# A transformer block on one core: where the last gate's row lies in the w_up stage, and how far ahead Pool makes its sums

## The chip, the cores and the metric

The kernel runs on one core of a Trainium2 chip. The core has a matrix engine (PE, with its weight loads shown apart as PEld), a vector engine (DVE), an activation engine (ACT), a general engine (POOL) and a queue engine (SP) that issues most of the DMAs. Each engine executes its own instructions strictly in the order in which the program lists them and waits on semaphores where it needs another engine's result. The metric is device microseconds of one execution; lower is better.

## The reference

One diffusion block in float32 over 1024 tokens of width 1024. What matters here is its second half, the feed-forward part, with 2816 hidden columns:

```python
def swiglu(h, w_up, w_down):
    a, b = jnp.split(h @ w_up, 2, axis=-1)
    return (jax.nn.silu(a) * b) @ w_down
...
        h2 = modulate(rmsnorm(x, g_ffn[l]), mod[:, 3, None], mod[:, 4, None])
        x = x + mod[:, 5, None] * swiglu(h2, w_up[l], w_down[l])
    return rmsnorm(x, g_final)
```

`mod[:, 5]` is the last gate, one row of 1024 numbers. The kernel multiplies it into the columns of w_down ahead of the product instead of into the result.

## The kernel before

Every float32 product is made of three fast matmuls: an operand is split into a high part (a copy on ACT, L92) and the rest (a subtraction on DVE, L93), and `mm3` (L121 to L123) adds high times high, high times low and low times high. Large products go through a Strassen scheme with seven products in place of eight. Its operands are blocks and sums of blocks, named B11, T2, T3, T1, B21, T4, B22.

The change lies in the w_up stage. It goes over 22 column blocks m of w_up, and each has seven products (five for the first four, which were begun earlier): 146 products of 12 matmuls. One written loop over products g sets the order of every engine's work, with nothing left to a scheduler. In turn g it issues:

- `up_sums`: POOL's sums of blocks of w_up for a product further ahead. T2 needs s1 and s2 (L1118, L1119), T3 needs s3 (L1123), B22 needs s4 (L1126). They lie in a ring of four buffers named st.
- `up_split` for product g + 4: the copy on ACT and the subtraction on DVE. After a block's last split the two loads of w_up for block m + 2 are issued on SP.
- the 12 matmuls of product g,
- work put off from earlier turns. The gate, one turn after a block's last product: a Silu on ACT (L1176), then a product on POOL (L1177). The stores of the result.
- `up_evac(g)`: DVE reads the product's bank (L1155 for T2, L1161 for T3, L1163 for T1, L1169 for T4, L1173 for B22). ACT reads B11 (L1153) and makes a Silu of B21 (L1166). T3 and T4 use one bank, so T4's matmuls must wait until L1161 has read T3.
- from block 3 on, a step or two of `DownOperands`. It prepares the operands of w_down for the stage after: rows are loaded (L809), multiplied by the last gate (L841, one row on DVE and one on POOL), combined, and each of seven forms is split into a tile named od (copy on ACT L813, subtraction on DVE L817), which SP stores to DRAM (L821). There are eleven pairs of rows. The forms come in the order B11, T2, B22, B21, T1, T3, T4; those of the last pair stay on chip.

The tiles od come out of a ring of 32 buffers of 4 KB per partition ("slots"). The stage holds 28 of them for the latents' operands and one for the last gate's row, m5, so that three rotate among the od tiles: a copy into od waits until the store of the tile three back has landed. Another ring, gl, has six buffers of half the size; the stage uses all six for the three tiles t per pair that carry T1, T3 and T4.

Of the kernel before, what the change touches and what calls it, by code (L numbers as in the profile page):

```python
# [12 lines left out]
ALU = mybir.AluOpType  # L13
# [22 lines left out]
HS = (H0, H1)  # L36
# [7 lines left out]
def block_kernel(ctx: ExitStack, tc: tile.TileContext,  # L44
# [4 lines left out]
    load, store = nc.sync.dma_start, nc.scalar.dma_start  # L49

    x, ctxt, out = x[0], ctxt[0], out[0]
# [13 lines left out]
    def slot(name, shape=(P, T), dtype=F32):  # L65
        return slots.tile(list(shape), dtype, name=name, tag="s", bufs=NS)
# [7 lines left out]
    def ev_(name="ev"):  # L74
        return wp.tile([P, HALF], F32, name=name, tag="ev", bufs=8)

    def gl_(name="gl"):
        return wp.tile([P, HALF], F32, name=name, tag="gl", bufs=6)
# [159 lines left out]
    def dtile(name, shape=(P, T)):  # L238
        return dram.tile(list(shape), F32, name=name)
# [6 lines left out]
    m5d = dtile("m5d")  # L246
# [469 lines left out]
    for n, (ka, fa, kb, fb) in enumerate(PAIRS):  # L716
# [23 lines left out]
        if ka[0] == "ff":  # L740
            e = ev_()
            zs = (e, c12, c21, c22)
# [44 lines left out]
    DPAIRS = [(ka, kb) for a, b in SEG for ka, kb in zip(a, b)]  # L787

    def last_gate():
        z = slot("m5")  # L790
        load(out=z, in_=m5d)
        return z

    class DownOperands:

# [37 lines left out]
        def one(self, i, j, m5):  # L833
            ra, rb = self.raw[i, 0], self.raw[i, 1]
            x11, x12, x21, x22 = ra[:, H0], ra[:, H1], rb[:, H0], rb[:, H1]
            t = self.t
            nxt = self.pairs.index(i) + 1
            nxt = self.pairs[nxt] if nxt < len(self.pairs) else None
            if j < 2:
                for eng, z in ((dve, ra), (pool, rb)):  # L840
                    eng.tensor_tensor(z[:, HS[j]], z[:, HS[j]], m5[:, HS[j]], op=ALU.mult)  # L841
            elif j == 2:
                t["T1"] = self.tile_("t")
                dve.tensor_tensor(t["T1"], x12, x11, op=ALU.subtract)
            elif j == 3:
                t["T3"] = self.tile_("t")
                dve.tensor_tensor(t["T3"], x22, x12, op=ALU.subtract)
                self.hi(i, "B11", x11)
            elif j == 4:
                dve.tensor_tensor(x12, x22, t["T1"], op=ALU.subtract)  # L850
            elif j == 5:
                self.lo(i, "B11")
                self.hi(i, "T2", x12)
            elif j == 6:
                t["T4"] = self.tile_("t")
                dve.tensor_tensor(t["T4"], x21, x12, op=ALU.subtract)
            elif j == 7:
                self.lo(i, "T2")
                if nxt is not None:
                    self.fetch(nxt, 0)  # L860
                self.hi(i, "B22", x22)
            elif j == 8:
                self.lo(i, "B22")
                self.hi(i, "B21", x21)
            elif j == 9:
                self.lo(i, "B21")
                if nxt is not None:
                    self.fetch(nxt, 1)
                self.hi(i, "T1", t["T1"])
            elif j < 12:  # L870
                nm, then = (("T1", "T3"), ("T3", "T4"))[j - 10]
                self.lo(i, nm)
                self.hi(i, then, t[then])
            else:
                self.lo(i, "T4")
# [171 lines left out]
    for h_ in range(2):  # L1047
# [16 lines left out]
        for n in range(4):  # L1064
            z = slot("xr")
# [3 lines left out]
        for k in range(4):  # L1069
            for m in (EARLY[k] if h_ else ()):  # L1070
                early.append(up_pair(m).head(True, m > 1, psum if m > 1 else None, gl_))
            if h_ == 0:
                fz = slot("F0", (P, 2, HALF))
                zs = [fz[:, 0, :], fz[:, 1, :]]
                F0.append(zs)
            else:
                zs = [ev_("z12"), ev_("z22")]
# [10 lines left out]
    LEAD = 4  # L1088
# [9 lines left out]
    def up_loads(m):  # L1098
        u = UP[m] = UpState()
        u.p = early[m] if m < len(early) else None  # L1100
        if u.p is not None and u.p.ra is not None:
            u.ra = u.p.ra
        else:
            u.ra = load_cols(w_up, m * P, KT)
        u.rb = load_cols(w_up, DFF + m * P, KT)
        u.o = {}
        u.a = dict(B11=u.ra[:, H0], B21=u.ra[:, H1], T4=u.rb[:, H1])

    def up_sums(g):
        m, nm = prods[g]  # L1110
        u = UP[m]
        a11, a12, a21, a22 = u.ra[:, H0], u.ra[:, H1], u.rb[:, H0], u.rb[:, H1]

        def st():
            return wp.tile([P, HALF], F32, name="st", tag="st", bufs=4)
        if nm == "T2":
            s1, s2 = st(), st()
            pool.tensor_tensor(s1, a21, a22, op=ALU.add)  # L1118
            pool.tensor_tensor(s2, s1, a11, op=ALU.subtract)  # L1119
            u.a["T1"], u.a["T2"] = s1, s2  # L1120
        elif nm == "T3":
            s3 = u.a["T3"] = st()
            pool.tensor_tensor(s3, a11, a21, op=ALU.subtract)  # L1123
        elif nm == "B22":
            s4 = u.a["B22"] = st()
            pool.tensor_tensor(s4, a12, u.a["T2"], op=ALU.subtract)  # L1126

    def up_split(g):
        m, nm = prods[g]
        UP[m].o[nm] = wop(UP[m].a[nm])  # L1130

    def up_product(g):
        m, nm = prods[g]
        u = UP[m]
        if nm in ("B11", "T2") and not hasattr(u, "bank"):
            p = u.p if u.p is not None else up_pair(m)
            u.bank = dict(zip("YZW", (f() for f in p.banks[1:])))
            u.bank["X"] = u.p.X if u.p is not None else p.banks[0]()
            u.m1 = u.p.m1 if u.p is not None else ev_("m1")
        ps = u.bank[dict(B11="X", T2="Y", T3="W", T1="Z", B21="X", T4="W", B22="Z")[nm]]  # L1140
        first = nm in ("B11", "T2", "T3", "T1")
        for k in range(4):
            mm3(ps, hl(u.o[nm], blk(k)), hl(G[nm][k]), first and k == 0, k == 3, not first)
# [4 lines left out]
    def up_evac(g):  # L1148
        m, nm = prods[g]
        u = UP[m]  # L1150
        b = u.bank
        if nm == "B11":
            act.copy(u.m1, b["X"])  # L1153
        elif nm == "T2":
            dve.tensor_tensor(u.m1, b["Y"], u.m1, op=ALU.add)  # L1155
            if u.p is not None:
                u.e = ev_()
                act.activation(u.e, b["X"], AF.Silu)
        elif nm == "T3":
            u.u3 = ev_("u3")  # L1160
            dve.tensor_tensor(u.u3, b["W"], u.m1, op=ALU.add)  # L1161
        elif nm == "T1":
            dve.tensor_tensor(u.u3, b["Z"], u.u3, op=ALU.add)  # L1163
        elif nm == "B21":
            u.e = ev_()
            act.activation(u.e, b["X"], AF.Silu)  # L1166
        elif nm == "T4":
            c21 = ev_("c21")
            dve.tensor_tensor(c21, b["W"], u.m1, op=ALU.add)  # L1169
            dve.tensor_tensor(u.e, u.e, c21, op=ALU.mult)  # L1170
            later(g + 1, lambda: store(out=Gd[m // 2][:, m % 2, H0], in_=u.e))
        else:
            dve.tensor_tensor(u.m1, b["Z"], u.m1, op=ALU.add)  # L1173

            def gate():
                act.activation(u.m1, u.m1, AF.Silu)  # L1176
                pool.tensor_tensor(u.m1, u.m1, u.u3, op=ALU.mult)  # L1177
            later(g + 1, gate)
            later(g + 2, lambda: store(out=Gd[m // 2][:, m % 2, H1], in_=u.m1))

    N = len(prods)
    made = DownOperands(list(range(1, len(DPAIRS))) + [0], gl_)
    first_made = prods.index((3, "T2"))
    with tc.manual_schedule():
        up_loads(0)
        up_loads(1)
        m5 = last_gate()
        for g in range(-LEAD - 1, N + 3):
            if 0 <= g + LEAD + 1 < N:
                up_sums(g + LEAD + 1)  # L1190
            if 0 <= g + LEAD < N:
                up_split(g + LEAD)
                m = prods[g + LEAD][0]
                if ends[m] == g + LEAD and m + 2 < NFF:
                    up_loads(m + 2)
            if 0 <= g < N:
                up_product(g)
            for fn in todo_at.pop(g, ()):
                fn()
            if 0 <= g < N:  # L1200
                up_evac(g)
            if g >= first_made:
                made.step((g + 1 - first_made) / (N + 2 - first_made), m5)
        made.step(1, m5)
# [154 lines left out]
    for s in range(len(SEG)):  # L1359
        segment(s, O, gs)  # L1360
        for t in RES.get(s, ()):
            for ch in range(2):
                z = gl_("xh")
# [32 lines left out]
```

## Time and profile before

| | us |
|---|---|
| median of 3 runs | 1546.57 (1545.77 to 1548.61) |
| the profiled execution | 1543.4 |
| its span, first instruction to last | 1541.7 |
| PE busy in the span | 1461.0 (95%) |
| DVE busy | 1127.9 (73%) |
| ACT busy | 715.5 (46%) |
| POOL busy | 600.9 (39%) |

A share of busy time is a mean over stages. In the rows below a stretch or an instruction is given by its start from the span's start. The bracket behind an instruction is the time for which its engine sat idle ahead of it, and what ended that.

### The profile page before, as it was taken

Reading aid. Unit: us, or ns where it says so; the run is one execution under the profiler, and the core shown is the slowest. Engines: PE = TensorE matmul, PEld = TensorE weight load, DVE = VectorE, ACT = ScalarE, POOL = GpSimd, SP = SyncE. Lnnn points to the kernel's source line nnn. Section 1 sums busy time; section 2 is a strip of 40 time slices with the busy share of each in tenths; the row PEclk is TensorE's granted clock in tenths of the full one; section 3 lists DMA queues with packets and bytes.
Section 4 is the critical chain, followed back from the end, with each engine's and each line's share of the span. In section 5 each row is a group of like instructions: output and inputs, shape, how many; then the busy total and the mean of one; then the engine's idle time right before and its main releaser. Section 6 shows DMA issues by size and latency. Waiting matters only on the chain.

```text
span 1541.7 us, 19297 instructions
## 1 busy us (share of the span) xinstructions
PE 1461.0 (95%) x6754; PEld 1196.2 (78%) x6754; DVE 1127.9 (73%) x1552; ACT 715.5 (46%) x1207; POOL 600.9 (39%) x402
## 2 busy tenths in 40 slices
PE   6998999999899999999999979999999999999997
PEld 6887788777677777888788757778778777788886
DVE  2456686888877657685736777888898889777786
ACT  4355655766433332234326543334343334767635
POOL 0033143434232224253512644445555454544456
PEclk9799999999999999999999989999999999999999
DMA  9343432334667748931645232566666656699922
GB/s 304 107 149 121 140 110 66 126 115 151 216 208 253 239 159 269 326 141 41 228 155 180 94 96 96 198 228 232 224 222 220 204 189 228 217 350 361 326 78 110
DMA packets 206931, 288.11 MB, mean 187 GB/s; under 512 B 11409, under 2 KB 131826, under 8 KB 206834
## 3 DMA queue, kind: packets, MB, share of 16 engines
q1 hardware_dynamic: 181778, 238.64, 47.5%
q10 hardware_dynamic: 25056, 48.25, 8.4%
q8 instruction: 53, 0.87, 0.2%
q14 instruction: 44, 0.36, 0.1%
HBM read 199.80 MB, written 87.03 MB: 186 GB/s over the span
## 4 chain that ended last, share of the span: by engine, by line
PE 46%; DVE 15%; issue 13%; DMA 11%; POOL 8%; ACT 6%; SPq 1%; ACTq 0%; POOLq 0%; DVEq 0%
PE acc L121 8%; PE acc L123 8%; PE acc L122 8%; DVE op L93 4%; PE aux L121 4%; PE aux L122 4%; PE aux L123 4%; DMA raw<-in_w_mod_dram 4%; PE aux L316 2%; DMA raw<-in_w_in_dram 1%; POOL rawd L841 1%; DMA OdB<-od 1%; ACT op L92 1%; DMA OdT<-od 1%; POOL st L1126 1%
## 5 line engine op out<-in xcount | busy, mean ns | idle before, releaser
L93 DVE TENSOR_TENSOR op<-raw,op 128x512 fp32r<-128x512 f32 x208 | 195.6, 945 | 100.6 <-ACT op L92 98.3
L92 ACT CAST op<-raw 128x512 fp32r<-128x512 f32 x216 | 131.7, 619 | 161.2 <-PE acc L123 99.9
L93 DVE TENSOR_TENSOR op<-st,op 128x512 fp32r<-128x512 f32 x160 | 144.4, 904 | 40.2 <-ACT op L92 39.3
L121 PE MATMUL acc<-T,op 128*128 128x512 f32 x400 | 159.9, 400 | 13.6 <-ACT T L92 6.1
L121 PE MATMUL aux<-T,op 128*128 128x512 f32 x400 | 158.5, 396 | 12.2 <-DVE u L1161 7.7
L92 ACT CAST op<-st 128x512 fp32r<-128x512 f32 x160 | 96.9, 618 | 146.3 <-POOL st L1119 27.3
L122 PE MATMUL acc<-T,op 128*128 128x512 f32 x400 | 159.2, 398 | 4.0 <-DVE T L93 4.0
L123 PE MATMUL acc<-T,op 128*128 128x512 f32 x400 | 157.9, 395 | 0.0
L122 PE MATMUL aux<-T,op 128*128 128x512 f32 x400 | 157.1, 393 | 0.0
L123 PE MATMUL aux<-T,op 128*128 128x512 f32 x400 | 156.2, 392 | 0.0
L121 PE MATMUL aux<-B,op 128*128 128x512 f32 x300 | 118.1, 394 | 5.9 <-DVE u L190 4.7
L121 PE MATMUL acc<-B,op 128*128 128x512 f32 x300 | 117.6, 393 | 3.0 <-ACT m L165 1.8
L123 PE MATMUL acc<-B,op 128*128 128x512 f32 x300 | 117.5, 392 | 1.6 <-DVE op L93 1.6
L122 PE MATMUL aux<-B,op 128*128 128x512 f32 x300 | 117.0, 390 | 0.0
L122 PE MATMUL acc<-B,op 128*128 128x512 f32 x300 | 116.9, 390 | 0.0
L123 PE MATMUL aux<-B,op 128*128 128x512 f32 x300 | 116.9, 390 | 0.0
L1177 POOL TENSOR_TENSOR m<-m,u 128x512 f32<-128x512 f32 x22 | 34.3, 1559 | 180.4 <-ACT m L1176 180.4
L121 PEld LDWEIGHTS acc<-T,op 128*128 128x128 f32 x400 | 76.5, 191 | 34.8 <-ACT T L92 8.0
L121 PEld LDWEIGHTS aux<-T,op 128*128 128x128 f32 x400 | 75.7, 189 | 33.2 <-issue 8.5
L181 POOL TENSOR_TENSOR st<-raw 128x512 f32<-128x512 f32 x18 | 32.6, 1812 | 170.3 <-DMA raw<-in_w_in_dram 127.3
L122 PEld LDWEIGHTS acc<-T,op 128*128 128x128 f32 x400 | 76.5, 191 | 21.3 <-DVE T L93 5.5
L123 PEld LDWEIGHTS acc<-T,op 128*128 128x128 f32 x400 | 76.3, 191 | 16.0 <-issue 0.2
(387 smaller groups left out, 3602.9 us busy)
## 6 DMA issues: line engine op xcount, KB each, us to landing
raw<-in_w_in_dram SPq DMA_DIRECT2D x60, 512.0 KB, 5.1
raw<-in_w_up_dram SPq DMA_DIRECT2D x46, 512.0 KB, 6.4
OdT<-od SPq DMA_DIRECT2D x40, 512.0 KB, 4.2
so<-OdT SPq DMA_DIRECT2D x40, 512.0 KB, 5.7
raw<-in_w_mod_dram SPq DMA_DIRECT2D x32, 512.0 KB, 4.9
OdB<-od SPq DMA_DIRECT2D x30, 512.0 KB, 4.9
so<-OdB SPq DMA_DIRECT2D x30, 512.0 KB, 6.5
rawd<-in_w_down_dram SPq DMA_DIRECT2D x22, 512.0 KB, 5.7
```

What stands on the lines that cost most here:

```text
L92: (act.copy if hi_eng is act else hi_eng.tensor_copy)(h, v)
L93: t_last[0] = lo_eng.tensor_tensor(l, v, h.bitcast(F32), op=ALU.subtract)
L121: pe.matmul(ps, lh, rh, start=first, stop=False, skip_group_check=cont)
L122: pe.matmul(ps, lh, rl, start=False, stop=False, skip_group_check=cont)
L123: pe.matmul(ps, ll, rh, start=False, stop=last, skip_group_check=cont)
L181: pool.tensor_tensor(s1, a21, a22, op=ALU.add)
L316: pe.matmul(ps[:, 2 * i:2 * i + 2], wm[f][i][:, blk(k)], sc[:, k, :], start=k == 0, stop=k == KT - 1)
L841: eng.tensor_tensor(z[:, HS[j]], z[:, HS[j]], m5[:, HS[j]], op=ALU.mult)
L1126: pool.tensor_tensor(s4, a12, u.a["T2"], op=ALU.subtract)
L1177: pool.tensor_tensor(u.m1, u.m1, u.u3, op=ALU.mult)
```

## The change

The last gate's row is loaded as two halves into two buffers of the ring gl, and later: two turns ahead of the first step of `DownOperands` instead of ahead of the loop. The slot that it held joins the rotation, so that the od tiles have four buffers in place of three, and the tiles t have four in place of six. POOL's sums are issued for product g + 6 in place of g + 5.

```diff
     def last_gate():
-        z = slot("m5")
-        load(out=z, in_=m5d)
-        return z
+        zs = [gl_("m5") for _ in HS]
+        for z, s in zip(zs, HS):
+            load(out=z, in_=m5d[:, s])
+        return zs
...
-                    eng.tensor_tensor(z[:, HS[j]], z[:, HS[j]], m5[:, HS[j]], op=ALU.mult)
+                    eng.tensor_tensor(z[:, HS[j]], z[:, HS[j]], m5[j], op=ALU.mult)
...
         up_loads(0)
         up_loads(1)
-        m5 = last_gate()
-        for g in range(-LEAD - 1, N + 3):
-            if 0 <= g + LEAD + 1 < N:
-                up_sums(g + LEAD + 1)
+        for g in range(-LEAD - 2, N + 3):
+            if g == first_made - 2:
+                m5 = last_gate()
+            if 0 <= g + LEAD + 2 < N:
+                up_sums(g + LEAD + 2)
```

The lists of PE, DVE and ACT stay as they were, name for name. POOL's list moves. From the gate of block 4 (L1177 on m1_7721) to the next gate it reads before as follows; st from L1126 is s4, from L1118 and L1119 s1 and s2, from L1123 s3, and L841 is the last gate's product with a half row of w_down:

```order
L1177 TENSOR_TENSOR m1_7721<-m1_7721,u3_7783 128x512
L841 TENSOR_TENSOR rawd_7811<-rawd_7811,m5_7267 128x512
L1126 TENSOR_TENSOR st_7905<-raw_7601,st_7790 128x512
L841 TENSOR_TENSOR rawd_7811<-rawd_7811,m5_7267 128x512
L1118 TENSOR_TENSOR st_7953<-raw_7769 128x512
L1119 TENSOR_TENSOR st_7954<-st_7953,raw_7767 128x512
L1123 TENSOR_TENSOR st_7974<-raw_7767,raw_7769 128x512
L1177 TENSOR_TENSOR m1_7886<-m1_7886,u3_7947 128x512
```

And after, POOL over the same stretch, with the sum s4 of the block before ahead of the gate (lines from here on stand one or two lower in the file):

```order
L1127 TENSOR_TENSOR st_7881<-raw_7607,st_7767 128x512
L1178 TENSOR_TENSOR m1_7725<-m1_7725,u3_7789 128x512
L842 TENSOR_TENSOR rawd_7815<-rawd_7815,m5_7559 128x512
L842 TENSOR_TENSOR rawd_7815<-rawd_7815,m5_7560 128x512
L1119 TENSOR_TENSOR st_7930<-raw_7775 128x512
L1120 TENSOR_TENSOR st_7931<-st_7930,raw_7773 128x512
L1124 TENSOR_TENSOR st_7959<-raw_7773,raw_7775 128x512
L1127 TENSOR_TENSOR st_8041<-raw_7773,st_7931 128x512
L1178 TENSOR_TENSOR m1_7890<-m1_7890,u3_7953 128x512
```

The sum s4 has moved from behind a gate to ahead of it, and behind the two L841 that stand there in other blocks. On SP, at the start of the stage, the gate's row stood between the second halves of the first two w_up blocks and the loads of the third:

```order
L103 DMA raw_7265<-in_w_up_dram 128x8x128
L791 DMA m5_7267<-m5d_156 128x1024
L103 DMA raw_7296<-in_w_up_dram 128x8x128
L103 DMA raw_7298<-in_w_up_dram 128x8x128
L103 DMA raw_7397<-in_w_up_dram 128x8x128
```

After, it comes in two halves behind the loads of block 4:

```order
L103 DMA raw_7265<-in_w_up_dram 128x8x128
L103 DMA raw_7296<-in_w_up_dram 128x8x128
L103 DMA raw_7298<-in_w_up_dram 128x8x128
L103 DMA raw_7397<-in_w_up_dram 128x8x128
L103 DMA raw_7399<-in_w_up_dram 128x8x128
L103 DMA raw_7501<-in_w_up_dram 128x8x128
L103 DMA raw_7503<-in_w_up_dram 128x8x128
L792 DMA m5_7559<-m5d_156 128x512
L792 DMA m5_7560<-m5d_156 128x512
L103 DMA raw_7607<-in_w_up_dram 128x8x128
```

Six loads of w_up have moved ahead of the gate's row. The only other move on SP is at the end of the stage, where the first load of a stored form (so, L1233) stands ahead of the last row of w_down and one od store instead of behind them.

## Rows read from the trace of the kernel before

**Rows 1.** Windows: busy us and (instructions) by engine, PE clock, DMA share, GB/s.

```profile
950.00:1000.00 50.00, 47.12 (x198) 38.28 (x199) 43.19 (x52) 18.81 (x34) 22.40 (x14) 0.97 0.49 172
...
1150.00:1200.00 50.00, 49.99 (x220) 40.83 (x219) 45.97 (x56) 19.63 (x35) 23.55 (x15) 1.00 0.66 220
...
1350.00:1400.00 50.00, 50.00 (x222) 41.20 (x221) 39.67 (x57) 36.17 (x46) 24.45 (x19) 1.00 0.99 351
```

**Rows 2.** The page: a matmul's group; count, busy us, mean ns, idle before.

```profile
L122 PE MATMUL aux<-B,op 128*128 128x512 f32 x300 | 117.0, 390 | 0.0
```

**Rows 3.** PE's waits from 900 to 1330: total us, times, longest.

```profile
PE aux L121 <- DVE u L1161: 7.7, 5, 2.2
...
PE acc L121 <- DVE u L1161: 2.8, 2, 2.2
PE acc L121 <- ACT op L1310: 2.3, 1, 2.3
PE acc L121 <- DVE u L1163: 1.1, 2, 0.7
```

**Rows 4.** Waits of all engines, 850 to 1320.

```profile
POOL m L1177 <- ACT m L1176: 179.7, 21, 14.8
ACT od L813 <- DMA OdT<-od: 49.5, 10, 9.9
ACT od L813 <- DMA OdB<-od: 42.2, 17, 6.2
DVE op L93 <- ACT op L92: 40.1, 19, 5.3
```

**Rows 5.** Timeline of PE, two resumptions.

```profile
950.30 0.47 PE L121 MATMUL aux<-T,op 128*128 128x512 f32 x1 [0.55 <-DVE u L1161]
...
991.49 0.47 PE L121 MATMUL aux<-T,op 128*128 128x512 f32 x1 [2.18 <-DVE u L1161]
```

**Rows 6.** Timeline of DVE ahead of the second.

```profile
967.50 0.68 DVE L93 TENSOR_TENSOR op<-raw,op 128x512 fp32r<-128x512 f32 x1
...
974.66 0.69 DVE L93 TENSOR_TENSOR op<-st,op 128x512 fp32r<-128x512 f32 x1 [5.28 <-ACT op L92]
...
976.18 0.69 DVE L93 TENSOR_TENSOR op<-st,op 128x512 fp32r<-128x512 f32 x1 [0.23 <-ACT op L92]
...
979.78 0.69 DVE L93 TENSOR_TENSOR op<-st,op 128x512 fp32r<-128x512 f32 x1 [0.98 <-ACT op L92]
980.39 0.68 DVE L1173 TENSOR_TENSOR m<-acc,m 128x512 f32<-128x512 f32 x1
...
983.90 1.77 DVE L93 TENSOR_TENSOR op<-raw,op 128x512 fp32r<-128x512 f32 x1
```

**Rows 7.** Timeline of ACT, same stretch.

```profile
973.49 0.62 ACT L813 CAST od<-t 128x512 fp32r<-128x512 f32 x1 [9.86 <-DMA OdT<-od]
```

**Rows 8.** Timeline of SP: store of the pair's first form; and of its second.

```profile
958.53 0.34 SPq L821 DMA_DIRECT2D OdB<-od  x1
...
965.81 1.96 SPq L821 DMA_DIRECT2D OdT<-od  x1
```

**Rows 9.** The tile od: its stores, from issue to landing.

```profile
DMA to landing us min/median/max: 2.6/4.5/8.7
```

**Rows 10.** Timeline of POOL: same stretch, and a late product on w_down's row.

```profile
981.82 1.61 POOL L1177 TENSOR_TENSOR m<-m,u 128x512 f32<-128x512 f32 x1 [14.79 <-ACT m L1176]
...
985.08 1.74 POOL L1126 TENSOR_TENSOR st<-raw,st 128x512 f32<-128x512 f32 x1
...
1256.92 2.55 POOL L841 TENSOR_TENSOR rawd<-rawd,m 128x512 f32<-128x512 f32 x2 [6.90 <-DMA rawd<-in_w_down_dram]
1265.09 1.61 POOL L1177 TENSOR_TENSOR m<-m,u 128x512 f32<-128x512 f32 x1 [5.63 <-ACT m L1176]
```

**Rows 11.** Windows of 10 us behind two of PE's waits.

```profile
990.00:1000.00 10.00, 8.51 (x30) 6.88 (x31) 9.92 (x14) 3.73 (x7) 3.49 (x3) 0.83 0.27 97
...
1130.00:1140.00 10.00, 7.79 (x28) 6.26 (x28) 9.94 (x13) 4.32 (x8) 4.29 (x3) 0.83 0.48 149
```

## The prediction

> **What bounds the kernel now.** Start with the table of windows. In the w_up stage PE is busy 49.99 of 50 us where nothing disturbs it, with 220 matmuls, so one starts every 0.227 us; in a disturbed window of the same length it starts 198 and its clock is 0.97 [rows 1]. PE is the bound, and only what it loses in this stage can be won. The groups of the page say that a matmul's record lasts 0.390 us [rows 2], 0.163 us longer than the distance to the next start, so each wait in the view of waits is really 0.16 us longer than shown.
>
> Then PE's waits. Two reasons make up the stage's loss: DVE's L1161, which must have read T3's bank before T4 may write it (7.7 + 2.8 us in seven waits), and L1163, the same for the other bank (1.1 us in two). Together 11.6 us in nine waits, with the correction 11.6 + 9 x 0.163 = 13.1 us [rows 3]. The next view is the clock behind the two longest of these waits: 0.83 over ten microseconds, twice [rows 11]. That is (1 - 0.83) x 10 = 1.7 us each, a short spell at 1.2 instead of 2.4 GHz after PE stood for some 2.2 us; together 3.4 us. So the stage holds 13.1 + 3.4 = 16.5 us at the most.
>
> Now why DVE reads late. DVE works for 43 to 46 of 50 us here [rows 1], so it cannot make up lost time quickly. In the timeline of DVE ahead of PE's wait of 2.18 us [rows 5] there is a hole of 5.28 us, which an ACT copy ended [rows 6]. ACT itself had stood for 9.86 us at a copy into od, until a store of an earlier od tile landed [rows 7]. Summed over the stage, ACT stands 49.5 + 42.2 = 91.7 us for od stores and DVE 40.1 us for ACT's copies [rows 4]. After the hole DVE reads block m's last bank (L1173) at 980.39; only then come the Silu and the gate on POOL, at 981.82 after 14.79 us of idling [rows 10]. Everything that POOL still owes stands behind that gate and comes in one burst. While POOL works, a DVE subtraction takes 1.77 us where it takes 0.68 us alone [rows 6]. So the lateness that ACT began is doubled by POOL's burst just ahead of L1161.
>
> **The change part by part.** *The fourth od buffer.* A copy into od now waits for the store four back. The copy at 973.49 is the pair's fifth; ACT was free for it at 973.49 - 9.86 = 963.63 [rows 7]. It waited for the second form's store, issued at 965.81; now it needs only the first's, issued at 958.53 [rows 8]. Stores land 2.6 to 8.7 us after issue [rows 9], so that one is there by 961.1 to 967.2: a wait of 0 to 3.6 us for 9.86. The sixth copy now meets the second's store, at the same 973.4, but ahead of it ACT has already made the fifth copy and the operand copy that DVE lacked. So DVE does in its hole the subtraction for the operand (0.69 us) and that for od (0.68 us by its like [rows 6]). The two later holes of 0.23 and 0.98 us came from ACT's catching up [rows 6] and go with it. L1173 comes 0.69 + 0.68 + 0.23 + 0.98 = 2.6 us sooner, and with it the gate and the burst. PE's wait there was 2.18 + 0.16 = 2.3 us: it goes, with 0.3 us to spare. The bounds for this part: none of the 16.5 us, if the wait only passes to the sixth copy, and all of it.
>
> *The sums a product earlier.* POOL's number of sums stays. But s4, 1.74 us, ran inside the burst at 985.08 [rows 10]; by the new list it stands ahead of the gate, in the 14.79 us in which POOL idled. That takes up to 1.77 - 0.68 = 1.09 us of slowed DVE work out of each burst, and s1 to s3 come a place earlier. Bounds: 0 and seven L1161 waits x 1.09 = 7.6 us; within the sum it serves the same waits as the buffer, so I add nothing for it.
>
> *What it costs.* The tiles t have four buffers for three a pair. A buffer is asked for again six steps after its last reader at the earliest (T3's at step 3 takes the buffer whose last reader was T1's step 10 of the pair before). There are 143 steps in 133 turns of 12 x 0.227 = 2.7 us, so that is 15 us, and I take nothing; without that cover DVE would stand. The gate's row is issued two turns, 5.4 us, or more ahead of its first reader, the first L841, and the median landing of a twice as large store is 4.5 us [rows 9]: nothing; at worst 8.7 - 5.4 = 3.3 us, once. On SP one more load stands ahead of the last row of w_down: its issue, and at worst its landing of up to 8.7 us by the stores, once, at the last pair, whose sums no longer stand behind that row; taken as nothing. Nothing is added to PE's, DVE's or ACT's lists.
>
> *The sum.* Not all of the 13.1 us goes. The first wait, 0.55 us at 950.30 [rows 5], has no od copy ahead of it; it is what a burst alone costs, a quarter of the 2.2 us of the large ones. I let a quarter of all stay: 13.1 x 0.75 = 9.8 us won. The clock's 3.4 us I count in full, since no wait near 2.2 us should be left. Gain 13.2 us: the profiled execution goes from 1543.4 to 1530.2 us. Before's median lies 3.17 us above that execution, so the forecast for the median is 1546.57 - 13.2 = 1533.4 us. The stage behind takes the gain over whole, since PE is busy 50.00 of 50 us there, though the DMA engines are at 0.99 [rows 1]. What is late next is DVE itself at 46 of 50 us. PE's 2.3 us at the stage's end, where the next stage's first operands are late (L1310) [rows 3], I leave as they are; they could go as well, since the loads of that stage queue on SP behind buffers that s4 frees.
>
> **The rivals.** *The burst alone decides.* POOL's work is not less, and each of its sums still makes a DVE subtraction 1.09 us longer [rows 6]. The Trainium skill ("SBUF — State Buffer", section "SBUF: two separate sides") calls the ports that the two share an exclusive lock: the later of two such instructions waits for all of the first. By that rule moving sums wins no DVE time at all, it only chooses which DVE instruction is hit. The trace's 0.68 and 1.77 us agree. As a mechanism here: the buffer brings nothing since DVE, slowed as much as before, falls behind in every burst; only s4's leaving shortens seven waits by half to all of 1.09 us, 3.8 to 7.6 us, middle 5.7, and the clock still falls: 1546.57 - 5.7 = 1540.9 us. For it speaks that a wait without any od copy exists (950.30). Against it, that the large waits follow a hole of DVE's. Chance 0.20.
>
> *The wait only moves.* The sixth copy waits for the landing at 973.4 as the fifth did, what stands behind it in ACT's list comes no sooner, and PE's waits stay within a microsecond or two: about 1545.5 us. For it: the store itself lands no earlier. Against it: five instructions are ahead of that landing now. Chance 0.12.
>
> *Slower: s4 behind late rows of w_down.* In the new list two L841 stand ahead of s4 in several blocks, and L841 waits for a row of w_down: at 1256.92 it had waited 6.90 us, and the gate came at 1265.09 [rows 10]. Between the end of that pair, 1256.92 + 2.55 = 1259.47, and the gate there are 5.6 us, of which s4 takes 1.74, so 3.9 us of slack. If a row lands over 3.9 us later, s4 and the gate behind it are late, then the split that needs s4, then DVE's reads. From the fastest to the slowest landing of an od store, as large as a row's load, there are 6.1 us [rows 9], so a late one costs 6.1 - 3.9 = 2.2 us; at four of ten pairs 8.8 us, less the 5.7 us of the burst: 1546.57 + 3.1 = 1549.7 us. Against it: for that the buffer must bring nothing, and SP is asked for nothing more. Chance 0.05.
>
> **How the numbers follow.** Most of PE's waits go: 0.63, at 1533.4 us. Its own range runs from all of it and the stage's end too, 1546.57 - 16.5 - 2.3 = 1527.8 us, to half of it, 1538. The range for 8 in 10 takes in the first rival and part of the second, 1528 to 1543.5 us. What a measurement of this kernel can tell from no change is 0.2%, 3.1 us. Faster by more: the forecast and nearly all of the first rival, 0.82; within it: the second and a rest, 0.12; slower: 0.06, the last rival and what I don't see.
>
> **What would show it.** Right: ACT's waits for od stores fall from 91.7 to below 50 us, DVE's for ACT's copies from 40.1 to below 25, PE's for L1161 from 10.5 to below 4; no window of the stage has a clock of 0.83; the sums s4 lie in POOL's idle time, and POOL's longest wait for the gate's Silu is shorter than 14.8 us. Wrong: PE's waits on L1161 of about 2 us still there behind bursts of POOL, with ACT's od waits gone (the first rival); ACT's od waits as long as before, now at the sixth copy (the second); ACT's copies waiting for s4 behind an L841 that waits for its row (the third). If PE's waits are gone and the time is not, the stage behind gave it back, and its waits would show where.

## The result, and the profile after

The changed kernel takes 1528.78 us (median of 4 runs, 1528.64 to 1530.2) against 1546.84 us for the kernel before on the same chip: a ratio of 0.9891, interval 0.9874 to 0.9907. It is 18 us faster; the forecast was 13.2. The profiled execution takes 1530.2 us with a span of 1528.5, 13.2 us less than the one of before, so that the sum, which was made against one profiled execution, came out to the tenth. That is in part luck, as the stage itself shows. Its first and last marks in PE's timeline stand below: PE's wait for T at the stage's entry and its wait for an operand of the next stage. First before (columns: start, duration, engine, line, operation, operands, and the idle time ahead with what ended it):

```profile
900.88 0.80 PE L121 MATMUL acc<-T,op 128*128 128x512 f32 x1 [3.16 <-ACT T L92]
...
1321.77 0.50 PE L121 MATMUL acc<-od,op 128*128 128x512 f32 x1 [2.31 <-ACT op L1310]
```

The same two of after, and between them the only two matmuls of PE that still wait:

```profile
902.75 0.80 PE L121 MATMUL acc<-T,op 128*128 128x512 f32 x1 [3.15 <-ACT T L92]
...
953.46 0.47 PE L121 MATMUL aux<-T,op 128*128 128x512 f32 x1 [0.55 <-ACT op L92]
...
1260.64 0.47 PE L121 MATMUL aux<-T,op 128*128 128x512 f32 x1 [1.87 <-DVE u L1162]
...
1307.86 0.60 PE L121 MATMUL acc<-od,op 128*128 128x512 f32 x1 [2.06 <-ACT op L1312]
```

From mark to mark the stage took 420.89 us and takes 405.11: 15.8 us less. The execution after entered the stage 1.9 us later than that of before and took 0.7 us more behind it, which leaves 13.2. A second profile of either kernel (below) gives 420.18 and 404.53 us, a difference of 15.7, while the entry of these four lies anywhere from 899.50 to 902.75. The stage's gain is thus firm, and the entry varies by itself.

The view of waits over the w_up stage answers to [rows 4], PE's part of it to [rows 3] (total us, times, longest):

```profile
POOL m L1178 <- ACT m L1177: 149.9, 22, 12.4
...
ACT od L814 <- DMA OdT<-od: 26.5, 8, 4.7
...
DVE op L93 <- ACT op L92: 23.9, 13, 4.0
...
ACT od L814 <- DMA OdB<-od: 9.8, 6, 4.1
...
PE aux L121 <- DVE u L1162: 1.9, 1, 1.9
```

ACT's waits for stores of od fell from 91.7 to 36.3 us, DVE's for ACT's copies from 40.1 to 23.9, PE's for the two banks from 12.0 to 1.9 (the prediction added up 11.6 and left out a line of 0.4). POOL's longest wait for the gate's Silu is 12.4 us, and the clock is 1.00 from 950 to the wait at the stage's end, so the signs that the prediction gave for being right are there. The windows answer to [rows 1]:

```profile
950.00:1000.00 50.00, 49.45 (x218) 40.62 (x217) 45.88 (x55) 18.40 (x33) 23.50 (x15) 1.00 0.50 174
...
1150.00:1200.00 50.00, 50.00 (x222) 41.39 (x221) 47.80 (x55) 20.92 (x38) 27.29 (x17) 1.00 0.61 200
```

The disturbed window holds 218 matmuls instead of 198, and its clock is 1.00 instead of 0.97. DVE works 45.88 of 50 us where it worked 43.19: it does the same work with fewer holes. How the first large wait of [rows 5] went can be followed along ACT, DVE and POOL; SP's issue of the second store of that pair is now at 967.81 where it was at 965.81 [rows 8], so some 2 us are to be taken off to compare places. ACT's timeline, the fifth and the sixth copy of the pair, answers to [rows 7]:

```profile
965.02 0.62 ACT L814 CAST od<-t 128x512 fp32r<-128x512 f32 x1
965.72 0.62 ACT L92 CAST op<-st 128x512 fp32r<-128x512 f32 x1
...
975.37 0.62 ACT L814 CAST od<-t 128x512 fp32r<-128x512 f32 x1 [1.95 <-DMA OdT<-od]
```

The fifth copy no longer waits, and the operand copy that DVE lacked follows it at once. The landing that the fifth met is now met by the sixth, after 1.95 us instead of 9.86. DVE's timeline answers to [rows 6], POOL's to [rows 10]:

```profile
976.54 0.69 DVE L93 TENSOR_TENSOR op<-st,op 128x512 fp32r<-128x512 f32 x1 [3.60 <-ACT op L92]
...
979.68 0.68 DVE L1174 TENSOR_TENSOR m<-acc,m 128x512 f32<-128x512 f32 x1
...
989.99 0.68 DVE L1162 TENSOR_TENSOR u<-aux,m 128x512 f32<-128x512 f32 x1
```

```profile
968.09 1.29 POOL L1127 TENSOR_TENSOR st<-raw,st 128x512 f32<-128x512 f32 x1 [0.69 <-DVE op L93]
...
981.11 1.60 POOL L1178 TENSOR_TENSOR m<-m,u 128x512 f32<-128x512 f32 x1 [11.73 <-ACT m L1177]
```

L1174 reads the last bank at 979.68, set back by those 2 us 977.7 where it was 980.39: 2.7 us sooner, where 2.6 were worked out. The sum s4 (L1127) has left the burst for POOL's idle time, as forecast. But from the gate to the read of T3's bank (L1162) there are 989.99 - 981.11 = 8.9 us, as before (990.67 - 981.82 = 8.9). Over the stage's blocks the median of this stretch is 7.2 us in both kernels. The wait went since all of this came sooner, not since the burst became shorter.

### The profile page after: what moved, and what is told of

Its sections match the earlier page's. It is cut to its first block, busy times and chain, and to the rows that moved or that the text cites. A ratio compares the mean times of both kernels' runs of the same rounds, so it can differ in the third digit from the quotient of the medians.

```text
span 1528.5 us, 19338 instructions
## 1 busy us (share of the span) xinstructions
PE 1459.4 (95%) x6754; PEld 1199.1 (78%) x6754; DVE 1131.6 (74%) x1552; ACT 714.4 (47%) x1207; POOL 599.4 (39%) x402
## 5 line engine op out<-in xcount | busy, mean ns | idle before, releaser
L92 ACT CAST op<-raw 128x512 fp32r<-128x512 f32 x216 | 131.9, 619 | 178.0 <-PE acc L123 105.2
L92 ACT CAST op<-st 128x512 fp32r<-128x512 f32 x160 | 96.8, 618 | 118.0 <-DVE ev L1171 20.0
```

Of the source, the lines that this page charges most:

```text
L92: (act.copy if hi_eng is act else hi_eng.tensor_copy)(h, v)
```

## The experiments

The length of the stage between the two marks serves beside the time, since it leaves out how late an execution enters it. Each time stands beside the kernel before on the same chip.

**e1_slot** and **e2_sums**: each part of the change alone. e1 takes the sums back to one product ahead; e2 is the kernel before with only the sums two ahead.

```diff
 # e1_slot, against after
-        for g in range(-LEAD - 2, N + 3):
+        for g in range(-LEAD - 1, N + 3):
-            if 0 <= g + LEAD + 2 < N:
-                up_sums(g + LEAD + 2)
+            if 0 <= g + LEAD + 1 < N:
+                up_sums(g + LEAD + 1)
 # e2_sums, against before
-            if 0 <= g + LEAD + 1 < N:
-                up_sums(g + LEAD + 1)
+            if 0 <= g + LEAD + 2 < N:
+                up_sums(g + LEAD + 2)
```

> The change without its second part: the last gate's row in two half-size buffers, four od buffers, POOL's sums one product ahead as before. Theory (ACT's waits for od stores start the chain, so the buffer carries the gain): most of it is here, 10 to 15 us of the changed kernel's 18 below before, so 1532 to 1537 us; ACT's waits for od stores fall to about 40 us as in the changed kernel, and PE's waits on DVE's L1161 fall from 10.5 to under 5 us. Rival (POOL's burst behind the gate decides, the buffer brings nothing): under 5 us below before, 1542 us or more, with PE's waits on L1161 still about 10 us although ACT's od waits are down.

> The change without its first part: POOL's sums two products ahead, the gate's row in its old slot, three od buffers. Theory: ACT's od waits stay at some 90 us and with them most of PE's waits; s4's leaving the burst wins 3 to 6 us, so 1541 to 1544 us. Rival (the burst decides): this carries the gain, 10 us or more, 1537 us or less, with ACT's od waits unchanged.

e1: 1527.61 us, 0.989 (0.9868 to 0.9911); e2: 1545.72 us, 1.0006 (0.9989 to 1.0024). The buffer alone brings the whole gain, more than the 10 to 15 us expected; the sums alone bring nothing that can be measured, where 3 to 6 us were expected. The waits of e1 are those of after, or lower:

```profile
DVE op L93 <- ACT op L92: 21.2, 15, 3.8
ACT od L814 <- DMA OdT<-od: 18.7, 9, 3.1
...
ACT od L814 <- DMA OdB<-od: 9.3, 5, 5.3
...
PE aux L121 <- DVE u L1162: 1.0, 2, 0.5
```

Why do the sums bring nothing, although s4 goes where it was sent? The timeline of DVE, POOL and PE in e2 ahead of a wait of 3.38 us:

```profile
1255.28 2.55 POOL L841 TENSOR_TENSOR rawd<-rawd,m 128x512 f32<-128x512 f32 x2 [8.70 <-DMA rawd<-in_w_down_dram]
...
1257.79 1.75 POOL L1126 TENSOR_TENSOR st<-raw,st 128x512 f32<-128x512 f32 x1
1258.31 1.79 DVE L817 TENSOR_TENSOR od<-t,od 128x512 fp32r<-128x512 f32 x1
...
1264.57 1.61 POOL L1177 TENSOR_TENSOR m<-m,u 128x512 f32<-128x512 f32 x1 [5.03 <-ACT m L1176]
...
1271.72 0.68 DVE L1161 TENSOR_TENSOR u<-aux,m 128x512 f32<-128x512 f32 x1
...
1272.54 0.47 PE L121 MATMUL aux<-T,op 128*128 128x512 f32 x1 [3.38 <-DVE u L1161]
```

At this place s4 (L1126) now runs just when DVE is catching up behind a hole, and makes that DVE subtraction 1.79 us long instead of 0.69. What the burst no longer costs, the catching up does. Over the whole stage that is not the full account, as the windows from mark to mark show, of before, of e2 and of after (DVE is the third of the busy times):

```profile
900.88:1321.77 420.89, 406.04 (x1749) 330.25 (x1749) 353.90 (x420) 158.45 (x285) 204.53 (x129) 0.99 0.58 195
```

```profile
900.97:1321.56 420.59, 406.00 (x1750) 330.44 (x1750) 348.54 (x420) 157.95 (x285) 198.69 (x129) 0.99 0.58 194
```

```profile
902.75:1307.86 405.11, 400.55 (x1749) 329.82 (x1749) 358.76 (x420) 157.63 (x285) 202.63 (x129) 0.99 0.61 203
```

For the same 420 instructions DVE is busy 5.4 us less in e2 than before, and the stage is no shorter; in after it is busy 4.9 us more, and the stage is 15.8 us shorter. What DVE loses to POOL in all is not what PE pays for.

**e3_held**: is it the buffer, or the gate's row in another ring? The changed kernel with one od slot held by a row that is loaded and stored back, read by nothing else: extra traffic of a load and a store.

```diff
                 m5 = last_gate()
+                held = slot("held")
+                load(out=held, in_=m5d)
 ...
             made.step(1, m5)
+        store(out=m2d, in_=held)
```

> The changed kernel with one slot held by a tile that is loaded where the gate's row is loaded and stored at the stage's end (0.5 MB each way, read by nobody), so that od tiles have three buffers again while the gate's row lies in the other ring and tiles t have four. Theory (it is the fourth od buffer, not where the gate's row lies): as the sums alone, 1541 to 1544 us, within 3 us of that run. If the later load of the row, or SP's freedom from it at the stage's start, had a part in the gain: nearer to the changed kernel than the sums alone, by 4 us or more.

1544.84 us, 1.0015 (0.9997 to 1.0033), with 52.0 + 45.5 us of od waits. With three buffers the gain is gone, within 1 us of e2 as expected. It is the fourth buffer.

**e4_sums3**, **e8_old_sums4**, **e7_sums4**: how far ahead the sums have to be to take POOL's burst away, and whether that alone would have done it. e4 and e7 are the changed kernel with the sums three and four products ahead, e8 the kernel before with four. In all three the edit is the number in the two lines shown for e1.

> The changed kernel with POOL's sums three products ahead. Theory (with four od buffers, what is left of PE's waits comes from late rows of w_down and od stores, not from the sums' place behind the gate): no change beyond 2 us, 1527 to 1531 us. Rival (the burst decides): s1 and s2 leave the burst behind the gate for the most part, the last waits on L1161 go too, 1524 to 1526 us. Above 1532 us if sums that wait for a buffer of the st ring hold up the gate.

> The kernel before, three od buffers, with POOL's sums four products ahead, so that s1 and s2 stand ahead of the gate as well as s4 and the burst behind it is the gate, s3 and products with w_down's rows. In the kernel before and with sums two ahead, from the gate's start to L1161 it is 7.16 and 7.15 us: s4's leaving shortened nothing, since gate, s1, s2 and s3 still cover that stretch. Theory A (PE waits only where a hole of DVE's and a burst come together; taking away either is enough): ACT's od waits stay at about 90 us and DVE's holes too, but gate to L1161 falls to 5 us or less and PE's waits on L1161 mostly go, so 1528 to 1534 us. Theory B (the hole alone makes DVE late, the burst matters little): PE's waits stay near 10 us and the time at 1542 to 1547 us.

> The changed kernel, four od buffers, with POOL's sums four products ahead. Theory A: both parts of the lateness are small now, PE's one wait of 1.9 us on L1161 goes as well and so may the one of 0.6 us at the start of w_down's steps, 1524 to 1527 us. Theory B: as the changed kernel, within 1.5 us. Slower than 1530 us if sums ahead of the gate wait for buffers of the st ring and hold the gate up.

e4: 1528.3 us, 0.9894 (0.9871 to 0.9917). POOL's waits for the Silu are 149.0 us there, as in after: s1 and s2 still stand behind the gate, against what was expected of the edit, so that e4 says nothing on the burst. With four they stand ahead of it. e8: 1550.68 us, 1.0024 (1.0007 to 1.0041), slower if anything and slower than both theories had it, its stage 425.95 us. e7: 1531.56 us, 0.9907 (0.9885 to 0.9929), no different from after within the intervals. The theory that either removal is enough gets no support: PE's waits on L1161 are 8.9 us in e8 where they were 10.5. But it is not refuted either, since the stretch from the gate to L1161 did not fall to the 5 us that the test asked for: its median over the blocks goes from 7.2 to 6.3 us. At the place where PE waits longest in e8 the burst is much shorter, as the timeline of DVE, POOL and PE shows:

```profile
1018.75 0.69 DVE L93 TENSOR_TENSOR op<-st,op 128x512 fp32r<-128x512 f32 x1 [5.15 <-ACT op L92]
...
1019.58 1.62 POOL L1118 TENSOR_TENSOR st<-raw 128x512 f32<-128x512 f32 x1 [4.83 <-DVE op L93]
1019.96 1.79 DVE L93 TENSOR_TENSOR op<-st,op 128x512 fp32r<-128x512 f32 x1
...
1026.27 1.61 POOL L1177 TENSOR_TENSOR m<-m,u 128x512 f32<-128x512 f32 x1 [3.10 <-ACT m L1176]
...
1032.45 0.68 DVE L1161 TENSOR_TENSOR u<-aux,m 128x512 f32<-128x512 f32 x1
...
1033.28 0.47 PE L121 MATMUL aux<-T,op 128*128 128x512 f32 x1 [2.98 <-ACT op L92]
```

From the gate to L1161 there are 6.2 us, where the same block has 8.9 before. But s1 (L1118) waits for DVE's first subtraction behind the hole and so runs in DVE's catching up, and PE waits 2.98 us all the same (the view names an ACT copy, which ended together with the read of L1161). Such waits of sums for DVE's subtractions come to 87.2 us in e8, where before has 1.8: with four buffers in the ring st, sums that far ahead wait for a subtraction to free one. Whether a larger ring st would let the sums run early enough was not tried. Removing the hole helps; moving POOL's sums within a list that is full of holes does not, as far as these runs go.

**e9_two**, **e10_five**: the number of od buffers taken further either way. e9 holds two slots as e3 held one. e10 adds a slot and takes the room from another ring; nothing is left out.

```diff
 # e9_two, against after
                 m5 = last_gate()
+                held = [slot("held") for _ in HS]
+                for z in held:
+                    load(out=z, in_=m5d)
 ...
+        for z in held:
+            store(out=m2d, in_=z)
 # e10_five, against after
-NS = 32
+NS = 33
-        return wp.tile([P, HALF], F32, name=name, tag="ev", bufs=8)
+        return wp.tile([P, HALF], F32, name=name, tag="ev", bufs=6)
```

> The changed kernel with two slots held (loaded where the gate's row is loaded, stored at the stage's end, 1 MB each way, read by nobody), so that od tiles have two buffers. Theory (a copy into od waits for the store so many buffers back, and ACT's list passes the wait on to DVE and PE): ACT's waits for od stores grow from 36 us with four and 92 with three to 150 us or more, and PE's loss with them, 1565 us or more: each buffer less costs more than the one before. If the gain came from something else that the fourth slot brought: within 3 us of the run with three buffers (1545).

> The changed kernel with five od buffers: the space of the fifth slot comes from the ring ev, which has six half-size buffers in place of eight throughout the kernel and may cost time in other stages, so that the stage's own rows count. ACT's waits for od stores fall from 36 to under 15 us. If what is left of PE's waits on L1161 in the changed kernel (1.9 us, once, behind od waits of 4.4 and 4.1 us) comes from them, it goes; the stage then ends about 2 us sooner after its start. If it comes from a late row of w_down, it stays at 1 to 2 us.

e9: 1601.61 us, 1.0343 (1.031 to 1.0376); e10: 1526.78 us, 0.9881 (0.9855 to 0.9907). The dose and its effect:

```
od buffers                    2        3        4        5
ACT's waits for od, us     153.3     91.7     36.3      5.1
median time, us           1601.6   1546.8   1528.8   1526.8
```

The waits are those of one profile each. Other profiles have 74.5 (e0, below), 90.4 (e2) and 97.5 us (e3) with three buffers, and from 28.0 to 40.9 with four. Waits of e9, from 850 to 1400 since its stage ends at 1378, and below of e10, to 1320 like the rest:

```profile
DVE op L93 <- ACT op L92: 100.7, 33, 8.3
ACT od L814 <- DMA OdB<-od: 84.9, 22, 9.6
ACT od L814 <- DMA OdT<-od: 68.4, 13, 10.4
...
PE aux L121 <- DVE u L1162: 20.6, 6, 6.0
```

```profile
DVE op L93 <- ACT op L92: 14.4, 20, 2.0
...
PE acc L121 <- ACT op L1312: 5.8, 1, 5.8
...
ACT od L814 <- DMA OdT<-od: 5.1, 5, 2.5
```

In e10 PE waits for L1162 no more. The 1.87 us that after still holds there was thus the od store's doing too: ahead of it two copies of after stand 4.39 and 4.13 us for landings. It differs between profiles with four buffers: 0.46 us in e1, from 1.34 to 2.41 in the five with earlier sums; whether the sums have a part in that is not shown.

```profile
1238.37 0.62 ACT L814 CAST od<-t 128x512 fp32r<-128x512 f32 x1 [4.39 <-DMA OdT<-od]
...
1243.12 0.62 ACT L814 CAST od<-t 128x512 fp32r<-128x512 f32 x1 [4.13 <-DMA OdB<-od]
```

But e10's wait at the stage's end grows from 2.06 to 5.8 us, and its stage is 406.00 us long, no shorter than after's. What comes before that wait is shorter, and the first operands of the next stage are not ready: the ring that gave up the room is the one that their loads use. In e11 below, where they use another, that wait is gone. The 2 us that were to come off the stage did not, and e10's median is no different from after's within the intervals.

**e5_early_g**, **e11_five_early**: the stage-end wait. e5 is the changed kernel with the first four loads of the next stage issued six products before the end, by a function of their own (left out below) into two buffers of the ring gl; e11 is e5 and e10 together. **e12_after_again** is the changed kernel beside e11 on one chip, **e0_before_again** a second profile of before.

```diff
+            if g == N - 6:
+                g00 = first_g()
 ...
-    gs, O = [load_g(0, 0)], made.kept
+    gs, O = [g00], made.kept
```

> The changed kernel with the first four loads of the next stage's weights issued six turns before the end of the w_up stage, into two buffers of the half-size ring that are free by then. In the changed kernel PE waits 2.1 us there for ACT's L1312, behind POOL's sums of these loads, and its clock is half for 3.4 us behind that. If the loads set that wait: 2 to 5 us less than the changed kernel, 1524 to 1527 us, PE's wait on L1312 gone and no half clock there. If ACT's own list at the stage's end sets it: no change within 1.5 us.

> The kernel before once more, for a second profile of it: all theories expect the same chain, some ten waits of PE on L1161 and L1163 and 85 to 100 us of ACT's od waits. How far the waits shift from one execution to another is what it shows; a span of 1540 to 1548 us.

> The two edits that took away what PE still loses, together on the changed kernel: five od buffers (ring ev with six buffers) and the next stage's first loads issued early into the half-size ring. With five buffers alone PE's wait at the stage's end grew to some 6 us, since those loads wait for the smaller ring ev; the early loads do not use it. If both act: no wait of over 1 us on L1161 and none of over 2 us at the stage's end, 1522 to 1525 us. If the stage behind gives it back (its stores and loads meet other waits): as either alone, 1526 to 1529 us.

> The changed kernel once more on the same chip as the run above, for comparison: 1527 to 1531 us, with one or two waits of PE on L1161 in the stage.

e5: 1528.09 us, 0.9882 (0.986 to 0.9905). The wait on L1312 is gone and the time is after's: four smaller waits, 3.3 us by the view, stand a few microseconds further on, where after has one of 1.2 us. Neither of its two theories holds: the loads did set that wait, and taking it away won nothing. PE's waits of e5 from 1295 to 1345:

```profile
PE acc L121 <- ACT X L1258: 1.1, 1, 1.1
PE acc L121 <- DVE X L1260: 0.8, 1, 0.8
PE acc L121 <- ACT B L1251: 0.7, 1, 0.7
PE acc L121 <- ACT T L1251: 0.7, 1, 0.7
```

e11: 1526.44 us, 0.9867 (0.9846 to 0.9888), and e12 on the same chip 1529.64 us, 0.9887 (0.9865 to 0.9909). e11 is the best version found by 3.2 us, short of the 1522 to 1525 us expected, and the intervals overlap; it stays open whether it beats the changed kernel. e0: 1542.18 us, with 39.6 + 34.9 us of od waits, less than the 85 to 100 expected, and the same chain. Single waits of PE lie elsewhere and differ by a microsecond or two; the stage's length, 420.18 against 420.89 us, repeats, and neither one wait nor the sum of ACT's does so well.

## Why the prediction was right, and where it was not

*The fourth od buffer* was right in mechanism, in place and in size. The fifth copy was to wait 0 to 3.6 us and waits none; L1173 was to come 2.6 us sooner and comes 2.7; e3 shows that three buffers undo it all, e1 that nothing else is needed.

*The sums a product earlier* were entered with nothing beside the buffer, and nothing is what they bring. The reason given, that each burst loses up to 1.09 us of slowed DVE work, did not hold. The stretch from the gate to L1161 is as long in after (8.9 us), and in e2 s4 slows another DVE instruction. The first rival drew from the exclusive lock on the ports that DVE and POOL share (the Trainium skill, "SBUF — State Buffer", section "SBUF: two separate sides") that moving sums wins no DVE time and only chooses which instruction is hit. At the place shown of e2 the trace agrees, a subtraction beside s4 takes 1.79 us instead of 0.69; over e2's whole stage it does not quite, since DVE is busy 348.54 us instead of 353.90. That time was won where PE does not wait for it: the stage stayed at 420.6 us.

*The quarter that stays* is the step that failed in its reason. It was taken because a wait of 0.55 us had no od copy ahead of it, so that every burst was held to cost a quarter. What stays is 0.55 us there and 1.87 at 1260.64, which is not far from the 3.3 us of the quarter; but the second is not a burst's price, it goes with a fifth buffer (e10). With five buffers the 0.55 us is all that PE waits for ahead of the stage's end, so the bursts cost next to nothing once DVE has no holes. Measured on the stage, the loss went by 15.7 to 15.8 us, where 9.8 + 3.4 = 13.2 was put down. A part of the 2.6 us beyond the sum has rows. The sum counted nine waits of PE, and the view has two more of 0.4 us each, L1163 on aux and ACT's L92. All eleven are 12.4 + 11 x 0.163 = 14.2 us, and after keeps 2.4 + 2 x 0.163 = 2.7: 11.5 won instead of 9.8. The wait at the stage's end is 0.25 us shorter. The rest was not traced to a row.

*The clock's 3.4 us* were won, as both windows of [rows 11] are at 1.00 in after, but the reason given for them does not hold. They were laid to the two longest waits, as if standing for some 2.2 us brought the fall. The longest of the nine is another one, and the clock behind it stayed at 1.00 (the wait, and the window over it):

```profile
1273.07 0.47 PE L121 MATMUL aux<-T,op 128*128 128x512 f32 x1 [2.24 <-DVE u L1161]
...
1272.00:1282.00 10.00, 8.93 (x39) 7.43 (x40) 9.97 (x17) 5.42 (x10) 1.97 (x2) 1.00 0.58 155
```

In e0 the clock is 1.00 from 910 to the stage's end, with waits of 2.43 and 2.27 us, and PE waits 14.3 us in fifteen waits where before has 12.4 in eleven: that kernel's stage is as long without the 3.4 us. That the term came out is thus in part luck. A spell like the two came behind the wait at the stage's end, in the window from 1308 to 1318 of after:

```profile
1308.00:1318.00 10.00, 10.00 (x38) 8.05 (x39) 6.87 (x15) 4.74 (x14) 4.86 (x6) 0.83 0.82 276
```

It costs (1 - 0.83) x 10 = 1.7 us. It is not the change's doing: the second profile of before has a clock of 0.83 from 1319 to 1329, behind the same wait, and the first has none.

*The costs taken as nothing* (the ring of t, the gate's row, SP's order) do not show: e3 has them all, and e2, with as many od buffers and the sums as far ahead, has none of the first two; their stages are 420.79 and 420.59 us long. *The stage-end wait* was left as it was, and is: 2.31 before, 2.06 after; e5 shows that taking it away alone gives nothing.

*The median.* It fell by 18 us where its sum said 13.2. Of the 4.8 us, some 2.6 were won in the stage beyond the sum. The rest is that single executions scatter: the profiled one of before is 3.4 us below its median, that of after 1.4 above. Runs of before in all sessions spread from 1539.96 to 1552.11 us, and its medians from 1544.12 to 1547.46, so a difference of two microseconds between sessions tells nothing.

*The rivals.* That the burst alone decides and the buffer brings nothing is refuted by e1, where the buffer alone brings it all, and by e2, where the sums alone bring nothing. That the wait only moves is true in a small part: the sixth copy waits 1.95 us in the place followed above, and 36.3 of 91.7 us of od waits are left. s4 behind late rows of w_down: POOL's waits for these rows do grow where sums stand ahead, from 8.4 to 17.4 us in e2 and 25.8 in e8, but in the changed kernel they are 5.9 us, and it is not slower.

## What to carry to other kernels

Where an engine that works through its list in order waits for a free buffer, what is lost is not its own idle time but the instructions behind it that others need; follow the hole from engine to engine, and count buffers by when the store lands, not by how many are in use on paper. Where POOL and DVE slow each other, moving POOL's work can save DVE time (5 us in e2) and win nothing: take away the hole that makes DVE catch up first. A gain in one stage is best read between two marks of that stage in the timeline, since executions of the same kernel enter it microseconds apart.

## What the runs showed that was not expected

The cost of too few buffers is far from linear: the third saves 55 us, the fourth 18, the fifth 2 at most, which is not clear of the noise (the kernels with held slots carry their extra loads and stores, which in e3 left the time at that of before). And PE's clock doesn't follow the length of a wait alone: behind the stage-end wait of 2.31 us the first profile of before stayed at 1.00 and the second, with 2.31 us as well, fell to 0.83 for one window. What else differs between the two is not shown. The second profile's window:

```profile
1319.00:1329.00 10.00, 9.32 (x34) 7.55 (x35) 7.66 (x15) 5.52 (x16) 5.48 (x7) 0.83 0.85 274
```
